# A hybrid decoder layer on one core: another rule for shared SBUF in the kernel's own planner, other planned durations, and three bias buffers in place of two

## The chip, the cores and the metric

The kernel runs on one core of a Trainium2 chip, in one launch. The metric is the device time of that launch in microseconds. The core has five instruction queues that run side by side and meet through semaphores: TensorE (PE; matmuls, with its weight loads shown as PEld), VectorE (DVE), ScalarE (ACT), GpSimd (POOL) and SyncE (SP, which here only issues DMAs). Each queue runs its instructions in the order in which the program issues them, so an instruction that waits holds up all that stand behind it on its engine.

## The reference

One layer on a sequence of 512 tokens with 1024 channels, in fp32. One input projection feeds two attention mixers; their outputs are gated, projected, merged and projected again:

```
h = rms_norm(x, norm_w);  proj = h @ w_in
q_a, k_a, v_a, z_a, q_b, kc, vc, ksl, vsl, kwn, vwn, gate_b, z_b, gate_m = split(proj)
o_a = moba_mixer(norm(q_a), norm(k_a), v_a, bias_a)              # 8 heads of 64
k_cmp = norm(compress(kc)); v_cmp = compress(vc)                 # 31 windows of 32 tokens, gelu MLP
o_b = nsa_mixer(norm(q_b), k_cmp, v_cmp, norm(ksl), vsl, norm(kwn), vwn, gate_b, bias_b)  # 8 heads, 2 groups
y_a = o_a * silu(z_a); y_b = o_b * silu(z_b); g_m = sigmoid(gate_m)
merged = g_m[:1024] * (y_a @ w_branch_a) + g_m[1024:] * (y_b @ w_branch_b)
out = x + merged @ w_out
```

At 512 tokens the block selections of both mixers take in every past block, so the first mixer is causal attention with a relative-position bias, and the second is the gated sum of three attentions with the same queries: over the 31 compressed windows, over the selected keys and over the window keys. The last two share the bias of their head.

## The kernel before

All products are made in fp32r with split operands: an operand is a rounded part (`wh`, `hh`, `ks`, `ph`: "hi") and the remainder (`wl`, `hl`, `kx`, `pl`: "lo"), and a product is three matmuls (hi hi, lo hi, hi lo; `mm3`, L382 to L396) or two. So every weight tile of 128x512 that SP loads (`wr`) costs a cast on ACT or POOL (L359, L363) and a subtraction on DVE or POOL (L368) before TensorE can use it.

Three streams of matmuls are mixed on TensorE: the projections, gates, branches and the output (`gemms`, L1575), the attention (`attention`, L1296: 24 units, one per head for the first mixer, two per head for the second, its branches `br` 0 and 1), and the compression (`cmp`). A unit makes scores of four row blocks (`qk`, L1011), adds the bias and takes the row maximum on DVE (L1045, output `P` or `p`, from PSUM), exponentiates on ACT (L1058), scales by the reciprocal sum on POOL, or for the first mixer on POOL or ACT (L1066, L1064), transposes on TensorE (L1076), splits the transposed block (`ph` on ACT, L1088, `pl` on DVE, L1090) and multiplies with the values (L1110, into `O`). Each head needs its bias matrix `T`, 128x512, loaded from a table in DRAM by `load_bias` (L807); the pool `T` has two buffers. For an NSA group (four heads) `pre0` (L1196) makes keys, queries and the scores over the compressed windows (`scp`, L1217), and `pre1` the transposes of their weights (`pct`, L1262).

**The planner.** No engine's order is written out by hand. While the program is built, a small model of the chip runs: it keeps a clock `now`, a time `free` at which each engine is next free, and a heap of chains of work. A `Chain` (L172) is a list of operations that follow each other, each with a cost in ns by engine: "A" ACT, "D" DVE, "P" POOL. Small letters mark how an operation uses the SBUF access that DVE and POOL share: "d" is a DVE operation with its inputs in SBUF, "P" a POOL operation that takes part in the same lock, "p" a POOL operation that waits for DVE's lock and takes none. `either(n)` (L160) leaves the choice between "d" and "P". `step` (L215) takes the chain with the earliest time, computes with `ends` (L163) when the operation would end on each engine that may do it, takes the earliest, and issues the instruction on that engine at once. `lock["d"]` and `lock["P"]` hold the end of the last such operation of each side; an operation that finds the other side's lock running is priced to end at that lock's end plus its own length less 55. The streams of matmuls are generators: each yields either a condition (a time, or None while unknown) or the length of what it has issued, and the loop at L1749 takes from those whose condition was met at least a margin ago (`margin`, 600 by default, `CMARGIN` for the compression) the one that has had the least of its share. So durations and locks in the model set the order of instructions on all engines and on SP, where the loads `dma` (L254) are issued in planned order too. Semaphores keep the result right whatever the real durations are.

`room(tag)` (L291) says when a buffer of a pool is free in the model, and `alloc` (L269) takes it; RES (L137) lists these pools with their sizes. The pool `att` (tag `a`) with NATT buffers of 128x512 is not in RES: its buffers are reused in turn. Weight tiles come through `NRAW` = 6 raw buffers.

Of the kernel before, what the change touches and what calls it, by code (L numbers as in the profile page):

```python
# [43 lines left out]
YA = {'g0': (0, 1), 'z1': (2, 3)}  # L44
SEQ = ("z0","g0","z1",0,4,"g1",1,5,"g2",2,6,"g3",3,7)
# [6 lines left out]
RAWS = (6, 48)  # L52
# [5 lines left out]
CMARGIN = 2500  # L58
PCT = 2500
# [48 lines left out]
def hybrid_kernel(ctx: ExitStack, tc: tile.TileContext, x, x0, xT, wtok, wchan, wz, wgate, gains, w1,  # L108
# [14 lines left out]
    def nm(s):  # L123
# [14 lines left out]
           "ph": (sp, 3), "P": (sp, 2), "p0": (sp, 2), "T": (sp, 2), "pf": (sp, 2)}  # L138
# [33 lines left out]
    class Chain:  # L172
# [42 lines left out]
        def step(c):  # L215
# [10 lines left out]
            if cost is None:  # L226
                fn()
            else:
                if now[0] > 30e3:
                    cost = {k: n * SLOW[k.upper()] for k, n in cost.items()}  # L230
                end, k = min((ends(k, c.t, n), k) for k, n in cost.items())
                wait = free[k.upper()] - 40 - c.t
                if wait > 0 and c.slack > 0:
                    c.slack -= wait
                    c.t += wait
                    c.push()
                    return
                if k in lock:
                    lock[k] = end
                free[k.upper()] = end  # L240
                c.t = end + OUT[k.upper()] + LAT
                fn(ENG[k])
# [73 lines left out]

    def later(f, d):
        def g():
            t = f()
            return None if t is None else t + d  # L320
        return g
# [252 lines left out]
    def sum_weights():  # L574
# [3 lines left out]
        def both(t, i, k, j, lead):  # L578
# [3 lines left out]
            Chain(t + lead).do({"p": 900}, lambda e: e.dma_start(out=o, in_=y, accum_op=ALU.add, max_dma_last_dim=2048))  # L582
# [236 lines left out]
    def compress_w(kv):  # L819
# [3 lines left out]
        def emit(ps):  # L823
# [10 lines left out]
            for i8 in range(2):  # L834
                XW = att("XW", F32).rearrange("p (i g c) -> p i g c", g=2, c=C32)
                ch.do({"p": 140}, lambda e, XW=XW: e.memset(XW[:, :, :, 31:32], 0.0))
                for g in range(2):
                    ch.do(either(248), lambda e, XW=XW, g=g, i8=i8: e.tensor_tensor(
                        XW[:, :, g, 0:31], b["X"][:, g, :].rearrange("p (c i) -> p i c", i=8)[:, :, i8:i8 + 31],
                        pos[:, kv, 8 * i8:8 * i8 + 8].unsqueeze(2).to_broadcast([P, 8, 31]), op=ALU.add),  # L840
                        (lambda: b["X"]) if i8 and g else None)
# [114 lines left out]
    def q_pair(box, name, col):  # L956
# [5 lines left out]
        for r, z in enumerate(qs):  # L962
            c.do({"A": 478}, lambda e, r=r, z=z: e.copy(z[0:64, :], pt[64 * r:64 * r + 64, :]))
        for r, z in enumerate(qs):
            c.do({"D": 602}, lambda e, r=r, z=z: e.tensor_sub(z[64:128, :], pt[64 * r:64 * r + 64, :], z[0:64, :].bitcast(F32)),
# [3 lines left out]
    def k_pair(boxes, name, col, firsts=None):  # L969
# [6 lines left out]
        for r, (ks, kx) in enumerate(kk):  # L976
            for i in range(2):
                c.do({"A": 478}, lambda e, r=r, z=ks[64 * i:64 * i + 64, :]: e.copy(z, pt[64 * r:64 * r + 64, :]))
        for r, (ks, kx) in enumerate(kk):
            c.do({"D": 602}, lambda e, r=r, ks=ks, kx=kx: e.tensor_sub(  # L980
                kx[0:64, :], pt[64 * r:64 * r + 64, :], ks[0:64, :].bitcast(F32)), pt if r else None)
        for r, (ks, kx) in enumerate(kk):
            c.do({"A": ca(512)}, lambda e, kx=kx: e.copy(kx[64:128, :], kx[0:64, :].bitcast(F32)))
# [9 lines left out]
    class Unit:  # L993
# [44 lines left out]
        def bias(u, c, b, sps, frees, T, last=False):  # L1038
# [10 lines left out]
            c.do({"D": cd(L)}, f, frees, "p0" if own else None)  # L1049
# [4 lines left out]
        def soft(u, c, b):  # L1054
# [12 lines left out]
            p = {"P": 315 + 0.834 * L}  # L1067
# [56 lines left out]
    def o_out(O, m, h):  # L1124
# [11 lines left out]
        ch.do({"A": 478}, f, None, "gmt")  # L1136
# [4 lines left out]
        ch.do({"D": 602}, f, lambda: z["t"])  # L1141
# [44 lines left out]
    def nsa_units(g):  # L1186
# [3 lines left out]
        def bias_now():  # L1190
            if ("T", 0) not in box:
                t = room("T")()
                if t is not None and t <= now[0]:
                    box["T", 0] = load_bias(8 + 4 * g)

        def pre0():  # L1196
            yield toks_of("kb")
            bias_now()
# [7 lines left out]
            bias_now()  # L1206
            yield need("cmpk")
            bias_now()
            sc = att("sc", F32).rearrange("p (i b c) -> p i b c", i=4, b=NT)
            for i in range(4):  # L1210
                q, qc = box["q"][i]
                yield qc.ready
                bias_now()
# [36 lines left out]
            if ("T", 0) not in box:  # L1250
                yield room("T")
                bias_now()

        def pre1():
            yield toks_of("vb")
            yield need("cmpv")
            yield later(box["pcc"].ready, PCT)
# [317 lines left out]
    def gemms():  # L1575
# [26 lines left out]
        pools = [alloc("T", "m", dt=F32R) for _ in range(2)] + [alloc("ph", "m", dt=F32R) for _ in range(3)]  # L1602
# [238 lines left out]
```

## Time and profile before

| | us |
|---|---|
| median of 3 runs | 452.92 (452.29 to 455.07) |
| the profiled execution, its own time | 452.21 |
| its span, first to last instruction | 450.1 |
| granted TensorE clock in it | 1.00 in every slice |
| HBM traffic | 282 GB/s over the span |
| bias loads `T` | 16, each 256 KB |

In the quoted rows a time without a unit is in microseconds. A row of the timeline has start, length, engine, line, operation, output<-inputs, size and count; brackets at its end show for how long its engine had been idle just before, and what ended that. A row of the costliest groups has the count, then busy time and the mean ns of one, then idle time before them and its releasers. A row of one line's instructions has minimum, median and maximum ns of one, then the first and last start. The letter q behind an engine means its queue, where DMAs are issued.

### The profile page before, as it was taken

To read this page: it belongs to the slowest core of one execution; us is meant where nothing else is said; L and a number is where in the kernel's file an instruction comes from. 1 tells how busy PE (TensorE), PEld (TensorE's weight loads), DVE (VectorE), ACT (ScalarE), POOL (GpSimd) and SP (SyncE) were. 2 spreads that over 40 slices of the span, in tenths; PEclk is the share of its full clock that TensorE was granted. 3 is DMA by queue.
4 is the path that set the end of the run, shared out by engine and by line. 5 is a ranking of instruction groups with operands and counts; after the bars stand their busy time and mean duration, and the time that the engine had idled before them with its cause. 6 is when DMAs were issued, how large, how long until landed. Compare 5 with 4: busy or idle time off the path is not lost.

```text
span 450.1 us, 8540 instructions
## 1 busy us (share of the span) xinstructions
PE 442.9 (98%) x2779; PEld 394.5 (88%) x2779; DVE 386.8 (86%) x949; ACT 302.4 (67%) x712; POOL 189.9 (42%) x226
## 2 busy tenths in 40 slices
PE   8999999999999999999899999999999999999996
PEld 7888888899888998889799999989899998998885
DVE  5999899889996789897899999889887699999873
ACT  6775778879998896657686856667664455555450
POOL 1254337747763454335565463647731051211000
PEclk9999999999999999999999999999999999999999
DMA  7886646878876869859967867958769979799862
GB/s 257 284 279 212 217 150 201 212 218 227 237 211 162 223 161 299 281 142 283 248 160 197 231 167 194 238 132 210 176 169 255 264 204 269 216 247 291 302 208 93
DMA packets 54220, 98.20 MB, mean 218 GB/s; under 512 B 5216, under 2 KB 8160, under 8 KB 54176
## 3 DMA queue, kind: packets, MB, share of 16 engines
q1 hardware_dynamic: 38944, 68.30, 47.0%
q0 software_dynamic: 7616, 14.68, 20.2%
q10 hardware_dynamic: 7616, 14.68, 9.8%
q8 instruction: 22, 0.36, 0.3%
q14 instruction: 22, 0.18, 0.1%
HBM read 90.69 MB, written 36.31 MB: 282 GB/s over the span
## 4 chain that ended last, share of the span: by engine, by line
PE 78%; DVE 11%; ACT 4%; issue 3%; DMA 3%; POOL 0%; SPq 0%; ACTq 0%; DVEq 0%
PE pgw L393 16%; PE pgt L393 14%; PE po L393 8%; PE pbr L393 8%; PE pgc L393 6%; PE O L1110 6%; PE pgf L675 5%; PE pt L1076 5%; DVE wl L368 3%; PE sps L1024 3%; PE sps L1025 2%; DMA wr<-in_wgate 2%; DVE P L1045 1%; DVE pl L1090 1%; ACT P L1058 1%
## 5 line engine op out<-in xcount | busy, mean ns | idle before, releaser
L368 DVE TENSOR_TENSOR wl<-wr,wh 128x512 fp32r<-128x512 f32 (+1 forms) x158 | 110.3, 713 | 4.1 <-ACT wh L359 2.9
L359 ACT CAST wh<-wr 128x512 fp32r<-128x512 f32 (+1 forms) x121 | 72.2, 611 | 15.9 <-DMA wr<-wsum 6.5
L1066 POOL TENSOR_SCALAR P<-P,sst,gate 128x512 f32<-128x512 f32 (+3 forms) x56 | 44.6, 799 | 57.8 <-DVE sst L1060 45.5
L363 POOL TENSOR_SCALAR wh<-wr 128x512 fp32r<-128x512 f32 (+1 forms) x48 | 38.2, 801 | 67.2 <-DMA wr<-wsum 20.0
L1058 ACT ACTIVATE P<-P,sst 128x512 f32<-128x512 f32 (+3 forms) x88 | 51.0, 580 | 11.6 <-DVE sst L1045 9.7
L393 PE MATMUL pgt<-wh,hh 128*128 128x512 f32 (+2 forms) x160 | 56.5, 353 | 0.4 <-DVE X L832 0.4
L393 PE MATMUL pgt<-wl,hh 128*128 128x512 f32 (+2 forms) x160 | 55.8, 349 | 0.0
L393 PE MATMUL pgt<-wh,hl 128*128 128x512 f32 (+2 forms) x160 | 55.7, 348 | 0.0
L1045 DVE CUSTOM_DVE_ANT_0 P<-sps,T 128x512 f32<-128x512 f32 (+3 forms) x88 | 43.9, 500 | 10.5 <-PE sps L1025 7.7
L393 PE MATMUL pgw<-th,wh 128*128 128x256 f32 x240 | 48.8, 282 | 0.1
L393 PE MATMUL pgw<-hh,wh 128*128 128x256 f32 x160 | 45.7, 285 | 0.2 <-ACT c L1472 0.2
L1088 ACT CAST ph<-pt 128x512 fp32r<-128x512 f32 (+2 forms) x72 | 33.6, 475 | 17.8 <-PE pt L1076 17.0
L393 PE MATMUL pgw<-hh,wl 128*128 128x256 f32 x160 | 44.4, 278 | 0.0
L393 PE MATMUL pgw<-hl,wh 128*128 128x256 f32 x160 | 44.4, 278 | 0.0
L1076 PE MATMUL pt<-cst,P 128*128 128x128 f32 x232 | 40.9, 273 | 0.5 <-POOL P L1066 0.5
L1090 DVE TENSOR_TENSOR pl<-pt,ph 128x512 fp32r<-128x512 f32 (+2 forms) x72 | 38.8, 548 | 2.3 <-ACT ph L1088 2.1
L393 PEld LDWEIGHTS pgw<-th,wh 128*128 128x128 f32 x240 | 39.1, 188 | 1.2 <-DVE gm L1531 0.5
L434 POOL TENSOR_TENSOR nr<-nss,mhalf 128x8 f32<-128x8 f32 (+1 forms) x16 | 28.7, 1792 | 25.1 <-DVE nss L433 19.5
L1076 PEld LDWEIGHTS pt<-cst,P 128*128 128x128 f32 x232 | 28.9, 140 | 5.5 <-POOL P L1066 0.9
L393 PEld LDWEIGHTS pgt<-wh,hh 128*128 128x128 f32 x160 | 30.1, 188 | 4.0 <-PE hps L862 0.5
L393 PEld LDWEIGHTS pgt<-wl,hh 128*128 128x128 f32 x160 | 30.1, 188 | 3.9
L393 PE MATMUL pgw<-th,wl 128*128 128x256 f32 x120 | 33.2, 277 | 0.0
(269 smaller groups left out, 1275.6 us busy)
## 6 DMA issues: line engine op xcount, KB each, us to landing
wr<-wsum SPq DMA_DIRECT2D x56, 256.0 KB, 4.9
wr<-in_wtok SPq DMA_DIRECT2D x36, 256.0 KB, 5.1
wsum<-in_wgate ACTq DMA_DIRECT2D x16, 512.0 KB, 4.8
wsum<-wsum POOLq DMA_DIRECT2D x14, 512.0 KB, 8.0
wr<-in_wgate SPq DMA_DIRECT2D x24, 256.0 KB, 4.7
xsum<-th SPq DMA_DIRECT2D x16, 256.0 KB, 2.4
T<-rtab SPq DMA_DIRECT2D x16, 256.0 KB, 4.7
wr<-in_w SPq DMA_DIRECT2D x16, 256.0 KB, 4.1
```

Source lines behind the costliest of these rows:

```text
L359: e.copy(hi, raw)
L363: e.tensor_scalar(hi, raw, 1.0, 1.0, op0=ALU.mult, op1=ALU.mult)
L368: c.do({"D": cd(n)} if lead else either(n), lambda e, hi=hi, lo=lo, raw=raw: e.tensor_sub(lo, raw, hi.bitcast(F32))).mark((w, 1, i))
L393: nc.tensor.matmul(dst, sts[i][a], mvs[i][b], start=(start and i == a == b == 0), stop=(stop and i == n - 1 and b == 1), skip_group_check= ...
L434: c.do({"p": 430 + POWC * w}, lambda e: e.tensor_tensor(v(dst), v(ss), mhalf[:parts, :w], op=ALU.pow))
L1045: e.tensor_tensor_reduce(u.block(b), sps[:, :L], T[:, S - L:], scale=-1.0, scalar=3e38, op0=ALU.add, op1=ALU.min, accum_out=st[:, 0, b:b + 1])
L1058: c.do({"A": 279 + 0.834 * L}, lambda e: e.activation(pv(), pv(), AF.Exp, bias=st[:, 0, b:b + 1], scale=-1.0, accum_out=st[:, 1, b:b + 1]))
L1066: e.tensor_scalar(pv(), pv(), st[:, 2, b:b + 1], g, op0=ALU.mult, op1=ALU.mult)
L1076: nc.tensor.transpose(pt[:, (b - kb) * P:(b - kb + 1) * P], u.p0 if u.p0 is not None and b == 0 else u.pb[:, POFF[b] + kb * P:POFF[b] + (k ...
L1088: e.copy(z["w"][0], pt[:, :w])
L1090: ch.do({"D": cd(w)}, lambda e: e.tensor_sub(z["w"][1], pt[:, :w], z["w"][0].bitcast(F32)), pt)
L1110: nc.tensor.matmul(O[0][:, S - n:], v.bitcast(F32) if kb == 3 else v, w, start=(u.first and kb == 0 and i == 0), stop=(u.last and kb == 3 ...
```

## The change

A planned operation that takes part in the lock and finds the other side holding it, while its own side's last such operation ended more than 30 ns before, is not issued: its chain goes back into the heap at the time at which the other side's lock ends, and engine and time are worked out anew then. Further operations of the other side may be planned in between and carry the lock on.

A number of planned durations get other values: two forms of split and copy between halves of the partitions, the addition `XW`, the POOL scaling, the bias operation. The accumulating DMAs that POOL issues get the kind "P" in place of "p", and 680 in place of 900 ns. CMARGIN goes from 2500 to 1000, and the extra delay of 2500 ahead of the transposes in `pre1` goes with its helper.

The pool `T` gets three buffers, `att` 47 in place of 48; the last stage uses the three `T` buffers as spare tiles in place of two. In `pre0` the bias of the group's first head is no longer loaded at the first of five places where a buffer is free, but once, at the end.

```
@@
-RAWS = (6, 48)
+RAWS = (6, 47)
...
-CMARGIN = 2500
-PCT = 2500
+CMARGIN = 1000
...
-           "ph": (sp, 3), "P": (sp, 2), "p0": (sp, 2), "T": (sp, 2), "pf": (sp, 2)}
+           "ph": (sp, 3), "P": (sp, 2), "p0": (sp, 2), "T": (sp, 3), "pf": (sp, 2)}
@@ step
                     c.t += wait
                     c.push()
                     return
+                o = "d" if k == "P" else "P"
+                st = max(c.t, free[k.upper()])
+                if k in lock and lock[o] > st + 1 and lock[k] < st - 30 :
+                    c.t = lock[o]
+                    c.push()
+                    return
                 if k in lock:
                     lock[k] = end
@@
-    def later(f, d):
...
@@ sum_weights
-            Chain(t + lead).do({"p": 900}, lambda e: e.dma_start(out=o, in_=y, accum_op=ALU.add, max_dma_last_dim=2048))
+            Chain(t + lead).do({"P": 680}, lambda e: e.dma_start(out=o, in_=y, accum_op=ALU.add, max_dma_last_dim=2048))
@@ compress_w
-                    ch.do(either(248), lambda e, XW=XW, g=g, i8=i8: e.tensor_tensor(
+                    ch.do({"d": 536, "P": cg(248)}, lambda e, XW=XW, g=g, i8=i8: e.tensor_tensor(
@@ q_pair
-            c.do({"A": 478}, lambda e, r=r, z=z: e.copy(z[0:64, :], pt[64 * r:64 * r + 64, :]))
+            c.do({"A": 590 if r else 482}, lambda e, r=r, z=z: e.copy(z[0:64, :], pt[64 * r:64 * r + 64, :]))
...
-            c.do({"D": 602}, lambda e, r=r, z=z: e.tensor_sub(z[64:128, :], pt[64 * r:64 * r + 64, :], z[0:64, :].bitcast(F32)),
+            c.do({"D": 715}, lambda e, r=r, z=z: e.tensor_sub(z[64:128, :], pt[64 * r:64 * r + 64, :], z[0:64, :].bitcast(F32)),
@@ k_pair
-                c.do({"A": 478}, lambda e, r=r, z=ks[64 * i:64 * i + 64, :]: e.copy(z, pt[64 * r:64 * r + 64, :]))
+                c.do({"A": 482 if i == r else 592}, lambda e, r=r, z=ks[64 * i:64 * i + 64, :]: e.copy(z, pt[64 * r:64 * r + 64, :]))
...
-            c.do({"D": 602}, lambda e, r=r, ks=ks, kx=kx: e.tensor_sub(
+            c.do({"D": 715 if r else 602}, lambda e, r=r, ks=ks, kx=kx: e.tensor_sub(
...
-            c.do({"A": ca(512)}, lambda e, kx=kx: e.copy(kx[64:128, :], kx[0:64, :].bitcast(F32)))
+            c.do({"A": 110 + ca(512)}, lambda e, kx=kx: e.copy(kx[64:128, :], kx[0:64, :].bitcast(F32)))
@@ Unit.bias, Unit.soft
-            c.do({"D": cd(L)}, f, frees, "p0" if own else None)
+            c.do({"D": cd(L) + 10}, f, frees, "p0" if own else None)
...
-            p = {"P": 315 + 0.834 * L}
+            p = {"P": 270 + 0.79 * L}
@@ o_out
-        ch.do({"A": 478}, f, None, "gmt")
+        ch.do({"A": 590}, f, None, "gmt")
...
-        ch.do({"D": 602}, f, lambda: z["t"])
+        ch.do({"D": 711 if row else 602}, f, lambda: z["t"])
@@ nsa_units
-        def bias_now():
-            if ("T", 0) not in box:
-                t = room("T")()
-                if t is not None and t <= now[0]:
-                    box["T", 0] = load_bias(8 + 4 * g)
...
-            bias_now()
...
-            if ("T", 0) not in box:
-                yield room("T")
-                bias_now()
+            yield room("T")
+            box["T", 0] = load_bias(8 + 4 * g)
...
-            yield later(box["pcc"].ready, PCT)
+            yield box["pcc"].ready
@@ gemms
-        pools = [alloc("T", "m", dt=F32R) for _ in range(2)] + [alloc("ph", "m", dt=F32R) for _ in range(3)]
+        pools = [alloc("T", "m", dt=F32R) for _ in range(3)] + [alloc("ph", "m", dt=F32R) for _ in range(3)]
```

More of the change, by code (lines that the diff above doesn't have):

```diff
@@ L43 @@
 YB = {"g3": (0, 1), 6: (2, 3)}
-YA = {'g0': (0, 1), 'z1': (2, 3)}
-SEQ = ("z0","g0","z1",0,4,"g1",1,5,"g2",2,6,"g3",3,7)
+YA = {"g0": (0, 1), "z1": (2, 3)}
+SEQ = ("z0", "g0", "z1", 0, 4, "g1", 1, 5, "g2", 2, 6, "g3", 3, 7)
 ASUM = 62e3
@@ L314, in all_of @@
         return f
-    def later(f, d):
[L318 to L321, printed above, removed]
     W1_ = [None]
@@ L1205, in pre0 @@
                 yield from q_pair(box["q"], "qb", 256 * g + P * i)
-            bias_now()
             yield need("cmpk")
-            bias_now()
             sc = att("sc", F32).rearrange("p (i b c) -> p i b c", i=4, b=NT)
@@ L1212, in pre0 @@
                 yield qc.ready
-                bias_now()
                 yield room("s")
@@ L1249, in pre0 @@
             box["pcc"] = cc
-            if ("T", 0) not in box:
-                yield room("T")
-                bias_now()
+            yield room("T")
+            box["T", 0] = load_bias(8 + 4 * g)
         def pre1():
```

## The prediction

> **What bounds the kernel now.** I read the page's shares first, then the chain that ended last, then the busy time by stage.
>
> ```profile
> PE 442.9 (98%) x2779; PEld 394.5 (88%) x2779; DVE 386.8 (86%) x949; ACT 302.4 (67%) x712; POOL 189.9 (42%) x226
> PE 78%; DVE 11%; ACT 4%; issue 3%; DMA 3%; POOL 0%; SPq 0%; ACTq 0%; DVEq 0%
> 0.00:4.72 4.72, 3.49 (x31) 3.25 (x32) 0.80 (x3) 2.29 (x4) 0.55 (x8) 1.00 0.59 148
> 4.72:60.00 55.28, 55.28 (x246) 45.54 (x247) 49.13 (x98) 37.93 (x76) 19.33 (x21) 1.00 0.76 255
> 60.00:200.00 140.00, 139.53 (x853) 122.38 (x853) 124.46 (x336) 114.39 (x277) 76.78 (x84) 1.00 0.78 213
> 200.00:240.00 40.00, 38.24 (x271) 34.86 (x270) 34.79 (x98) 29.23 (x80) 23.83 (x31) 1.00 0.77 204
> 240.00:400.00 160.00, 159.76 (x1156) 149.11 (x1155) 141.48 (x354) 98.81 (x244) 66.50 (x80) 1.00 0.81 213
> 36.04 0.39 PE L393 MATMUL pgt<-wl,hh 128*128 128x512 f32 x1
> 36.27 0.39 PE L393 MATMUL pgt<-wh,hh 128*128 128x512 f32 x1
> ```
>
> The second line is the share of each engine in the chain, the next five are stages (length, then busy PE, PEld, DVE, ACT, POOL, the granted clock, the DMA share and GB/s). TensorE is the bound, at the full granted clock. Its idle time between the first weights and the last stage is 140.00-139.53 = 0.47, 40.00-38.24 = 1.76 and 160.00-159.76 = 0.24: 2.47 us. The last two rows say that this is too little: neighbouring matmuls start 0.23 us apart while each is shown 0.39 long, so every wait is 0.16 longer than its idle row, and waits under 0.16 don't show. With some fifteen waits (an estimate) the whole is about 2.5 + 15 x 0.16 = 5 us. That is all a better order of instructions can win: the change leaves the matmuls, the head and the last products alone. What it can lose has no such limit. The profiled execution took 452.21 us: 450.1 of span and 2.1 around it. The median of the three runs, 452.92, is 0.7 above it.
>
> **The change, part 1: who holds SBUF.** Nothing is added to the program; the planner orders it differently. A planned operation of kind "d" or "P" that finds the other engine holding SBUF, and whose own engine has not just used it, is now put off to the end of that hold and chosen anew; before, it was issued at once and priced as starting 55 ns before that end. Is the hold real?
>
> ```profile
> 366.80 3.24 POOL L363 TENSOR_SCALAR wh<-wr 128x512 fp32r<-128x512 f32 x1 [4.43 <-DVE ma L1368]
> 366.66 0.69 DVE L368 TENSOR_TENSOR wl<-wr,wh 128x512 fp32r<-128x512 f32 x1
> 368.87 0.69 DVE L368 TENSOR_TENSOR wl<-wr,wh 128x512 fp32r<-128x512 f32 x1
> 370.74 1.84 POOL L363 TENSOR_SCALAR wh<-wr 128x512 fp32r<-128x512 f32 x2
> 370.83 1.27 DVE L1524 TENSOR_TENSOR gm<-gm,R 128x512 f32<-128x512 f32 x1
> 372.03 1.09 DVE L368 TENSOR_TENSOR wl<-wr,wh 128x512 fp32r<-128x512 f32 x1
> L363 POOL TENSOR_SCALAR wh<-wr x48: 592/622/3241, 7.7 to 400.8; 128x512 fp32r<-128x512 f32 x45, 128x280 fp32r<-128x280 f32 x3
> ```
>
> The same POOL operation has a median of 622 ns and once took 3.24 us: while six DVE operations with both inputs in SBUF (the first and the last are shown) followed each other without a gap, it did not get in once. Where POOL itself came straight from another operation (370.74, two in 1.84), the engines took turns: DVE's 1.27 and 1.09 are a 0.69 operation and a wait for POOL. The new test, with its exception for an engine that has just held SBUF, says both. [...]
>
> What the better price is worth is seen where TensorE waits.
>
> ```profile
> 216.49 1.30 POOL L368 TENSOR_TENSOR wl<-wr,wh 128x512 fp32r<-128x512 f32 x1
> 216.87 1.47 DVE L368 TENSOR_TENSOR wl<-wr,wh 128x512 fp32r<-128x512 f32 x1
> 218.26 0.41 DVE L1045 CUSTOM_DVE_ANT_0 P<-sps,T 128x256 f32<-128x256 f32 x1
> 218.60 0.88 DVE L1090 TENSOR_TENSOR pl<-pt,ph 128x384 fp32r<-128x384 f32 x2
> 219.20 0.44 PE L1110 MATMUL O<-pl,vb 128*128 128x384 f32 x1 [0.84 <-DVE pl L1090]
> 219.65 1.55 POOL L1066 TENSOR_SCALAR P<-P,sst,gate 128x384 f32<-128x384 f32 x2 [1.87 <-DVE sst L1060]
> 221.26 0.55 PE L1076 MATMUL pt<-cst,P 128*128 128x128 f32 x3 [0.54 <-POOL P L1066]
> ```
>
> POOL held SBUF from 216.49 to 217.8; DVE's split at 216.87 was queued behind it and blocked, and with it the bias and `pl` behind it on DVE, which read PSUM and needed no part of the hold. TensorE then waited 0.84 for `pl`. With the new test that split is put off to 217.8 and the two go first, 1.4 us earlier: the 0.84 goes. The other 0.92 of the 1.76 is of mixed cause (0.54 is a POOL scaling), and I take half: -0.84-0.46 = -1.30. Of the 0.47+0.24 elsewhere I take half, -0.35, and 3 waits x 0.16 hidden, -0.48. What is late next is DVE: 34.79 of 40 us busy there, so a plan that orders it otherwise cannot empty it. Bounds of this part: -5 (all waits) to 0, or above: it can also push POOL's work to DVE and ACT. If all twelve splits that POOL now makes (the row below) went to DVE at 0.69 each, that is 8.3 us, against 400-350.7 = 49 us of DVE idle time before 400 (0.80+49.13+124.46+34.79+141.48 = 350.7): covered, except at 200-240, where each would cost up to its 0.69.
>
> ```profile
> L368 POOL TENSOR_TENSOR wl<-wr,wh x12: 783/1300/2396, 66.5 to 271.3; 128x512 fp32r<-128x512 f32 x9, 128x280 fp32r<-128x280 f32 x3
> ```
>
> **Part 2: measured durations.** They change no instruction, only the plan's clock.
>
> ```profile
> L965 DVE TENSOR_TENSOR qs<-pq,qs 64x512 fp32r<-64x512 f32 x16 | 11.0, 690 | 1.6 <-ACT qs L963 1.2
> L963 ACT CAST qs<-pq 64x512 fp32r<-64x512 f32 x16 | 9.3, 582 | 2.7 <-PE pq L947 2.5
> L1066 POOL TENSOR_SCALAR P<-P,sst,gate 128x512 f32<-128x512 f32 x16 | 14.5, 903 | 38.9 <-DVE sst L1060 26.7 <-PE sps L1025 8.3 <-PE pt L1076 3.6
> L582 POOL DMA_DIRECT2D wsum<-wsum x14 | 12.9, 921 | 5.3 <-DMA wsum<-wsum 5.3
> ```
>
> 602 becomes 715 (row: 690), 478 becomes 482 or 590 (582): nearer. The scaling goes from 742 to 674 at 512 columns, further from 903; POOL's DMA issue from 900 to 680 (row: 921), and it now takes part in the hold. I set this part to 0: right in two, wrong in two. At most each of the 28 issues (the loops of `sum_weights`) plans POOL 0.2 early, 5.6 us in all, on an engine that is 42% busy; the lower end is the same with the sign turned.
>
> **Part 3: three bias buffers, loads later.** The early load in `pre0` (`bias_now`, five places) goes; the bias of each NSA group is now asked for behind all scores, and a third buffer takes the place of one of 48 in the pool `att`.
>
> ```profile
> T<-rtab SPq DMA_DIRECT2D x16, 256.0 KB, 4.7
> DMA to landing us min/median/max: 3.7/4.7/7.5
> 196.38 5.03 SPq L256 DMA_DIRECT2D T<-rtab  x2
> 169.03 0.53 SPq L256 DMA_DIRECT2D T<-rtab  x1
> 178.17 1.13 PE L1217 MATMUL scp<-kcs,qs 128*128 128x64 f32 x8
> 181.76 0.69 DVE L1045 CUSTOM_DVE_ANT_0 P<-sps,T 128x512 f32<-128x512 f32 x1
> 240.80 0.53 SPq L256 DMA_DIRECT2D T<-rtab  x1
> 259.76 0.53 PE L1217 MATMUL scp<-kcs,qs 128*128 128x64 f32 x4
> 262.93 0.69 DVE L1045 CUSTOM_DVE_ANT_0 P<-sps,T 128x512 f32<-128x512 f32 x1
> 250.00:275.00 25.00, 24.96 (x180) 23.24 (x179) 24.03 (x70) 19.09 (x51) 14.29 (x16) 1.00 0.71 178
> ```
>
> Gain: with two buffers a bias load stood at the head of SP's queue from 196.4 to 200.9 until DVE released a buffer, and the weight loads behind it stood too. TensorE did not wait for a weight there, so I count 0. Loss: the groups' first biases were loaded at 169.03 and 240.80, 12.7 and 22.1 us ahead of use at 181.76 and 262.93. Behind the last scores (end about 179.1 and 260.1) plus 4.7 they land at 183.8 and 264.8: 2.0 and 1.9 late if the rest stays where it is. DVE's bias waits, and behind it on DVE the weight splits that TensorE needs some tiles later. After 250 DVE has 25.00-24.03 = 0.97 idle in 25 us, so 0.9 of the second can come through; I take +0.5. Bounds: 0 (the plan has other work first) to what the longest landing gives, 179.1+7.5-181.8 = 4.8 and 260.1+7.5-262.9 = 4.7. The one `att` buffer less I set to 0: the last stage gets it back as a third spare tile; the bound is one reload held back, 4.7 by the nearest load row.
>
> **Part 4: two margins.** The compression matmuls may now start 1.0 instead of 2.5 us after the plan thinks their input is ready, and the extra 2.5 ahead of the transposes `pct` goes, so an error of the plan reaches TensorE sooner.
>
> ```profile
>   DVE vl L368: 0.2, 1
>   ACT ch L954: 4.9, 2
> ```
>
> These are the compression's only wait for DVE, 0.2 us once, and the followers of `pct` (ACT, 4.9 in two waits, nobody's bound). Sixteen weight tiles at up to 0.2 are 3.2 us; I take +0.3, and 0 as the lower end.
>
> **Sum**, against 452.21: -1.30-0.35-0.48+0.5+0.3 = -1.33, so 450.9. From the median of 452.92 the same step gives 451.6. I forecast between them: 451.2 us.
>
> **Rivals.** (a) All waits go: 452.2-5 = 447.2. For it: the largest waits lie in one stage with a cause that the new test names. Against: DVE is 87% busy there and causes most of them. (b) The change does not do what it says: the holds over several operations hit nothing on the path (at 366.80, where POOL lost 2.6 us, stage 240-400 has 0.24 of TensorE idle in all), and the new order wins and loses alike: 452.5. [...] (c) Slower: the late bias at the start of the NSA groups takes the place of the waits removed. At the longest landing the two are 4.8 and 4.7 late. DVE can make up 0.97 of the second, and of the first 2.8 (its idle share in 60-200 is 15.5 of 140, over 25 us): 2.0+3.7 = 5.7, with nothing won, 457.9. It decides once the plan puts the first NSA bias less than a landing behind the last score; for it speaks that DVE runs in order and nothing but that bias guards its place, against it that the plan itself adds about 2.7 us for this load, so only the rest is a surprise.
>
> **How the numbers follow.** Forecast (half the waits go, 449.5 to 452.2) 0.46; (a) 0.08; (b) 0.24; (c) 0.22, half of it near its full price. The range reaches to (a) and to (c): 447.6 to 456.8 leaves 2 in 10 out; the likeliest case alone has 449.5 to 452.2. About 1%, 4.5 us, is what can be told from no change here. Faster by over that (below 448.4): (a) and a little of the forecast, 0.12. Slower (over 457.4): 0.15, from (c) and from orders that I don't see. Within: 0.73.
>
> **What would show it.** Right: in the stage around 200-240 TensorE's idle time falls from 1.76 to below 1; no POOL operation of 0.6 takes over 2 us; DVE has fewer splits of over 1 us; the last two bias loads of a group stand no longer at SP's head. Wrong: idle time of DVE ahead of the bias line L1045 just behind the scores, ended by a DMA of `T`; new TensorE waits on `vl` or `pcs`; a TensorE idle sum above 2.5 us outside the head and the last stage.

## The result and the profile after

The changed kernel takes 457.92 us (median of four, 457.38 to 460.36), the kernel before 452.87 beside it: a ratio of 1.0112, with a 95% interval of 1.0084 to 1.014. It is 5.05 us slower, where 451.2 was forecast. The profiled execution took 458.30, with a span of 456.4 against 450.1. In the code after the change lines up to about L1190 stand one lower than before, later ones twelve lower.

The busy time by engine, from the page of the profile:

```profile
PE 442.2 (97%) x2779; PEld 394.1 (86%) x2779; DVE 387.0 (85%) x950; ACT 302.7 (66%) x709; POOL 187.8 (41%) x228
```

Every engine is busy for as long as before, within 2.1 us. What grew is TensorE's idle time, from 7.2 us (450.1-442.9) to 14.2 (456.4-442.2); that covers the 6.3 us of span. By stage (start:end, length, then busy time of PE, PEld, DVE, ACT, POOL, clock, DMA share, GB/s):

```profile
4.72:60.00 55.28, 54.63 (x247) 44.88 (x247) 48.17 (x100) 38.28 (x77) 17.90 (x19) 1.00 0.77 258
60.00:200.00 140.00, 134.81 (x821) 118.02 (x820) 121.88 (x323) 107.82 (x261) 76.05 (x88) 1.00 0.77 210
200.00:240.00 40.00, 38.38 (x270) 35.35 (x269) 33.80 (x102) 30.24 (x84) 25.50 (x31) 1.00 0.75 198
240.00:400.00 160.00, 158.52 (x1142) 147.54 (x1141) 139.56 (x350) 100.67 (x245) 64.35 (x79) 1.00 0.80 208
```

Idle time is length less busy time: 0.65, 5.19, 1.62 and 1.48, where it was 0, 0.47, 1.76 and 0.24. The sum, outside the head and the last stage, is 8.94, where it was 2.47. The stage on which the forecast rested, 200 to 240, gained 0.14; the one that had nothing left to win, 60 to 200, lost 4.72. What TensorE waited for, before (engine, tile, line, releaser: us in all, times, longest):

```profile
PE O L1110 <- DVE pl L1090: 1.2, 2, 0.8
PE pw L456 <- POOL ones L407: 0.9, 1, 0.9
PE pt L1076 <- POOL P L1066: 0.5, 1, 0.5
PE pgt L393 <- DVE X L832: 0.4, 1, 0.4
PE pgf L675 <- DVE wh L361: 0.4, 1, 0.4
PE pgw L393 <- ACT c L1472: 0.2, 1, 0.2
```

The same view after the change:

```profile
PE pt L1075 <- POOL P L1065: 2.3, 2, 1.6
PE pt L1075 <- DVE sst L1059: 1.9, 2, 1.6
PE sps L1023 <- DVE sst L1044: 1.7, 1, 1.7
PE pt L1075 <- DVE qs L964: 1.0, 2, 0.7
PE pw L455 <- POOL ones L406: 0.9, 1, 0.9
PE hps L862 <- DVE vl L367: 0.7, 1, 0.7
PE pgf L674 <- POOL wh L362: 0.6, 1, 0.6
PE pgw L392 <- ACT c L1460: 0.6, 1, 0.6
PE pgf L674 <- DVE wh L360: 0.2, 1, 0.2
PE pt L1075 <- DVE kx L979: 0.2, 1, 0.2
```

The sums are 3.6 and 10.1, so 6.5 more, about the 6.3 of the span. The two waits for `pl` (1.2), the ones the change was to remove, are gone. In their place stand waits of the transposes `pt` for POOL's scaling or for an operation of DVE (`sst`, `qs`), of the scores `sps` for DVE, and of `hps` for a weight split. The waits that DVE ends went from 2.0 to 5.7. The timeline shows how the three longest come about:

```profile
90.92 0.95 POOL L581 DMA_DIRECT2D wsum<-in_wz  x1
91.62 1.58 POOL L367 TENSOR_TENSOR vl<-wr,vh 128x512 fp32r<-128x512 f32 x1
91.43 2.07 DVE L367 TENSOR_TENSOR wl<-wr,wh 128x280 fp32r<-128x280 f32 x1
94.51 0.38 PE L1023 MATMUL sps<-ks,qs 128*128 128x256 f32 x1 [1.75 <-DVE sst L1044]
163.65 1.60 POOL L367 TENSOR_TENSOR wl<-wr,wh 128x512 fp32r<-128x512 f32 x1
164.02 1.77 DVE L367 TENSOR_TENSOR vl<-wr,vh 128x512 fp32r<-128x512 f32 x1
168.45 0.52 PE L1075 MATMUL pt<-cst,P 128*128 128x128 f32 x3 [1.62 <-DVE sst L1059]
221.06 5.67 POOL L1065 TENSOR_SCALAR P<-P,sst,gate 128x384 f32<-128x384 f32 x3 [1.19 <-DVE sst L1059]
223.67 1.88 DVE L367 TENSOR_TENSOR wl<-wr,wh 128x512 fp32r<-128x512 f32 x3
226.04 0.55 PE L1075 MATMUL pt<-cst,P 128*128 128x128 f32 x3 [1.62 <-POOL P L1065]
```

In the first two a DVE split ends just behind the POOL split beside it, at 93.50 us (POOL at 93.20) and at 165.79 (POOL at 165.25): 2.07 us for an operation whose shortest row on this line is 0.42, 1.77 for one with a median of 0.68. The next DVE operations start at 93.43 and 165.83 us, so the bias operation (93.77) and the sums (168.22) come late, and TensorE stands. In the third it is the other way round: three POOL scalings take 5.67 where the mean of their line is 862 ns, and three splits follow each other on DVE meanwhile. So the contention that the new test was to plan around stands behind the three longest waits of the new order, 5.0 of the 10.1; whether they would go without it is asked further down, with the order held fixed. The experiments ask whether the test, another part, or the redrawing of the order itself brought it.

### The profile page after: what moved, and what is told of

Same layout as the page of the kernel before. It is cut to its first block, busy times and chain, and to the rows that moved or that the text cites. A ratio compares the mean times of both kernels' runs of the same rounds, so it can differ in the third digit from the quotient of the medians.

```text
span 456.4 us, 8530 instructions
## 1 busy us (share of the span) xinstructions
PE 442.2 (97%) x2779; PEld 394.1 (86%) x2779; DVE 387.0 (85%) x950; ACT 302.7 (66%) x709; POOL 187.8 (41%) x228
## 4 chain that ended last, share of the span: by engine, by line
PE 81%; DVE 9%; DMA 5%; POOL 2%; issue 2%; ACT 1%; SPq 0%; ACTq 0%; DVEq 0%
PE pgt L392 18%; PE pgw L392 17%; PE pbr L392 9%; PE po L392 8%; PE pgc L392 6%; PE O L1109 5%; PE pt L1075 4%; PE pgf L674 4%; PE sps L1023 3%; PE sps L1024 2%; POOL P L1065 2%; DMA wr<-in_wgate 2%; DVE P L1044 1%; DMA xsum<-th 1%; DVE vl L367 1%
## 5 line engine op out<-in xcount | busy, mean ns | idle before, releaser
L367 DVE TENSOR_TENSOR wl<-wr,wh 128x512 fp32r<-128x512 f32 (+1 forms) x158 | 107.5, 698 | 2.0 <-ACT wh L358 1.1
L358 ACT CAST wh<-wr 128x512 fp32r<-128x512 f32 (+1 forms) x125 | 74.2, 610 | 16.5 <-DMA wr<-in_wtok 4.4
L1065 POOL TENSOR_SCALAR P<-P,sst,gate 128x512 f32<-128x512 f32 (+3 forms) x56 | 47.8, 862 | 57.0 <-DVE sst L1059 42.0
L362 POOL TENSOR_SCALAR wh<-wr 128x512 fp32r<-128x512 f32 (+1 forms) x44 | 35.0, 802 | 68.2 <-PE pgw L392 27.6
L433 POOL TENSOR_TENSOR nr<-nss,mhalf 128x8 f32<-128x8 f32 (+1 forms) x16 | 26.9, 1682 | 23.8 <-DVE nss L432 18.1
L392 PEld LDWEIGHTS pgt<-wh,hl 128*128 128x128 f32 x160 | 30.1, 188 | 3.3
```

The source lines that it names most:

```text
L358: e.copy(hi, raw)
L362: e.tensor_scalar(hi, raw, 1.0, 1.0, op0=ALU.mult, op1=ALU.mult)
L367: c.do({"D": cd(n)} if lead else either(n), lambda e, hi=hi, lo=lo, raw=raw: e.tensor_sub(lo, raw, hi.bitcast(F32))).mark((w, 1, i))
L392: nc.tensor.matmul(dst, sts[i][a], mvs[i][b], start=(start and i == a == b == 0), stop=(stop and i == n - 1 and b == 1), skip_group_check= ...
L433: c.do({"p": 430 + POWC * w}, lambda e: e.tensor_tensor(v(dst), v(ss), mhalf[:parts, :w], op=ALU.pow))
L1065: e.tensor_scalar(pv(), pv(), st[:, 2, b:b + 1], g, op0=ALU.mult, op1=ALU.mult)
```

## The experiments

The change has four parts: **M**, both margins (`CMARGIN` and the delay ahead of `pct`); **H**, the test who holds SBUF; **T**, three bias buffers with the late load; **D**, the durations. Without M none of the other three was tried on the kernel before. Each time is a median beside runs of the kernel before on the same chip (452.6 to 453.7), with the ratio to it and its interval.

### The parts

Before with M, alone and with one part beside it. The first edit:

```
-CMARGIN = 2500
+CMARGIN = 1000
...
-            yield later(box["pcc"].ready, PCT)
+            yield box["pcc"].ready
```

> Before with the two margins alone (compression 1000 in place of 2500, no extra 2500 ahead of the transposes pct). Theory 'hold' (the loss of 5.05 us comes from the new rule for SBUF, which puts POOL and DVE against each other at the wrong places): no change, 452 to 454 us. Theory 'any new order' (the order of before was a lucky one, and whatever makes the planner order anew loses some us): slower, 455 to 459. Theory 'margin' (matmuls issued before their input is there): slower by most of the 5, 456 to 458, with TensorE waiting on vl in the compression.

Measured: 462.23, ratio 1.02 [1.0162, 1.0238].

With H besides:

```
+                o = "d" if k == "P" else "P"
+                st = max(c.t, free[k.upper()])
+                if k in lock and lock[o] > st + 1 and lock[k] < st - 30 :
+                    c.t = lock[o]
+                    c.push()
+                    return
```

> Before with the margins and the new rule for SBUF. Theory 'hold': close to the changed kernel, 456 to 460 us, with DVE operations of over 1.7 us behind POOL and POOL scalings of over 2.2 us. Theory 'any new order': slower than before, 454 to 460, without relation to the first. Theory 'late bias': as the margins alone, 452 to 454.

Measured: 457.85, ratio 1.0109 [1.0073, 1.0146].

M with T (the pools, and `bias_now` gone; some of its lines):

```
-RAWS = (6, 48)
+RAWS = (6, 47)
...
-            if ("T", 0) not in box:
-                yield room("T")
-                bias_now()
+            yield room("T")
+            box["T", 0] = load_bias(8 + 4 * g)
...
```

> Before with the margins and the three bias buffers with their late load. Theory 'late bias': 456 to 458 us, with DVE idle ahead of the bias line at the start of the two NSA groups, ended by a DMA. Theory 'hold': as the margins alone, 452 to 454. Theory 'any new order': 454 to 460.

Measured: 465.77, ratio 1.0293 [1.0228, 1.0358].

M with D (all the durations; one for the rest):

```
-            p = {"P": 315 + 0.834 * L}
+            p = {"P": 270 + 0.79 * L}
```

> Before with the margins and the new durations (with the lock for POOL's DMA issues). Theory 'hold': as the margins alone, 452 to 454 us. Theory 'any new order': 454 to 460. A theory 'too cheap scaling' (POOL's scaling planned 0.07 us shorter, so the transposes are issued too soon): slower by 2 to 4, with TensorE waiting on POOL's scaling.

Measured: 457.83, ratio 1.0105 [1.0074, 1.0137].

From the other end, the changed kernel without T, and then without D (one line for the rest in each):

```
-           "ph": (sp, 3), "P": (sp, 2), "p0": (sp, 2), "T": (sp, 3), "pf": (sp, 2)}
+           "ph": (sp, 3), "P": (sp, 2), "p0": (sp, 2), "T": (sp, 2), "pf": (sp, 2)}
```

> The change without its third part: two bias buffers, 48 buffers in att, the early bias load. Theory 'late bias' (that part costs, as from 462.2 to 465.8 between the kernels with the margins alone and with the margins and the biases): 453 to 456 us. Theory 'any new order' (each order is a draw, about 452 to 466, and only a part's mean over several orders means something): 453 to 463, on either side of the changed kernel's 457.9.

Measured: 461.63, ratio 1.0192 [1.0152, 1.0232].

```
-            p = {"P": 270 + 0.79 * L}
+            p = {"P": 315 + 0.834 * L}
```

> The change without the new durations (and with the old lock for POOL's DMA issues). Set against the kernel with margins and biases (465.8) it shows the rule for SBUF once more: theory 'the rule helps' (with the margins alone it brought 462.2 to 457.9): 459 to 463 us, with less blocked time of DVE and POOL than there. Theory 'hold' (the rule is the loss): 466 or more. Theory 'any new order': 453 to 466.

Measured: 462.98, ratio 1.0219 [1.0176, 1.0263].

What follows: beside M, none of the other parts has a price of its own, or even a sign. H takes 4.4 from M alone (462.23 to 457.85) and 2.8 from M with T (465.77 to 462.98), but adds 3.8 to M with D (457.83 to 461.63). D takes 4.4 from M and 5.1 from M with H and T (462.98 to 457.92), but adds 3.8 to M with H. T adds 3.5 to M and takes 3.7 from M with H and D. By the intervals such a difference is known to some 2 to 4 us, so the 2.8 could be nothing, and T's 3.5 only just is not; the changes of sign of H and of D are clear. The differences do not add up.

### The margins

They are the two values that every run so far shares. One at a time on the kernel before: `CMARGIN` alone, then the delay alone.

```
-CMARGIN = 2500
+CMARGIN = 1000
```

> Before with the compression's margin alone, 1000 in place of 2500. Theory 'compression margin' (the 8.5 us that both margins cost come from compression matmuls that are issued too early): 459 to 463 us. Theory 'transposes' (they come from the extra delay of 2500 that is gone): 452 to 454. Theory 'any new order': 455 to 460, like any other edit.

Measured: 460.88, ratio 1.0179 [1.0135, 1.0222].

```
-            yield later(box["pcc"].ready, PCT)
+            yield box["pcc"].ready
```

> Before without the extra 2500 ahead of the transposes pct, the compression's margin kept. TensorE's order is the same up to some 190 us. Theory 'compression margin': 452 to 454 us. Theory 'transposes': 459 to 463, with TensorE waiting at the first pct. Theory 'any new order': 454 to 460.

Measured: 450.12, ratio 0.9951 [0.9932, 0.9971]: faster than both kernels. Up to about 200 us its TensorE order is that of before. In its profile two of the waits between 200 and 240 us are gone (TensorE is idle there for 0.80 instead of 1.76), but three new ones stand behind 360, so where its 2.5 us come from stays open.

So the margin of the compression seemed to be the loss. If it is, a value between must lie between, and the changed kernel with nearly the old margin must be near the time before:

```
-CMARGIN = 1000
+CMARGIN = 2300
```

> The changed kernel with the compression's margin at 2300 in place of 1000. Theory 'compression margin': TensorE's waits at 80 to 175 us fall to the 3 us of the kernel before, and the time to 452 to 455 us. Theory 'any new order': 455 to 465, with waits anywhere.

Measured: 460.61, ratio 1.017 [1.0149, 1.0192].

The kernel before, with a margin a fifth smaller:

```
-CMARGIN = 2500
+CMARGIN = 2000
```

> Before with the compression's margin at 2000 in place of 2500. Theory 'compression margin': little of the 8.2 us that 1000 costs, so 453 to 456 us, with the extra waits at 100 to 150. Theory 'any new order': 455 to 462, with waits anywhere.

Measured: 463.54, ratio 1.0228 [1.021, 1.0246].

So the price does not follow the size of the margin. Giving back most of it makes the changed kernel 2.7 slower, and on the kernel before a margin of 2.0 us costs more (463.54) than one of 1.0 (460.88). Nor do the compression's own matmuls `hps` stand among TensorE's waits in the run with `CMARGIN` alone; the largest there are waits of `pt`, 1.8 for POOL's scaling and 1.7 for `qs`. One thing is not excluded: that any shorter margin costs some us on the average, by way of the order. All twelve redrawn orders here that have one, at 1.0, 2.0 or 2.3 us, take 457.83 or more, and no run has H, T and D with the old margin.

### Edits that mean nothing

If any redrawing costs, an edit with no physical content must cost as well. Four of them: the planned start of the weight sums 0.1 us later, on both kernels; the planned length of the small power operation on POOL longer by 5 ns per column (it has 4 or 8 columns); a latency constant of the plan 2 ns longer.

```
-ASUM = 62e3
+ASUM = 62.1e3
```

> Before with the weight sums planned 0.1 us later (62.1 in place of 62): an edit that means nothing, and orders TensorE's instructions anew from the first quarter on. Theory 'any new order': 455 to 460 us. All other theories: 452 to 454.

Measured, on the kernel before: 454.95, ratio 1.0053 [1.0033, 1.0072].

```
-POWC = 180
+POWC = 185
```

> Before with POOL's power planned 5 ns longer per column: again an edit that means nothing, and a new order from the first tenth on. Theory 'any new order': 455 to 460 us, and not the same as the other nudge. All other theories: 452 to 454.

Measured, on the kernel before: 458.76, ratio 1.0112 [1.0067, 1.0157].

```
-ASUM = 62e3
+ASUM = 62.1e3
```

> The changed kernel with the weight sums planned 0.1 us later, an edit that means nothing. Theory 'any new order': other than 457.9 by 1 to 5 us, on either side. Theory 'the parts set the time': 457 to 459.

Measured, on the changed kernel: 462.36, ratio to the kernel before 1.0188 [1.0146, 1.0231].

```
-LAT = 60
+LAT = 62
```

> The changed kernel with each planned hand-over between engines 2 ns longer, an edit that means next to nothing and orders nearly everything anew. Theory 'any new order': other than 457.9 by 1 to 5 us, on either side. Theory 'the parts set the time': 457 to 459.

Measured, on the changed kernel: 464.37, ratio 1.0249 [1.0191, 1.0306].

These nudges cost 2.3 and 6.1 us on the kernel before (from 452.63) and 4.4 and 6.5 on the changed one. The change's own 5.05 is of that size, and 20 to 40 ns in one planned duration give the same ratio, 1.0112; that the two ratios agree to the last digit is chance. All the redrawn orders together, the changed kernel among them, are fifteen: from 450.12 to 465.77, with a median of 460.88. One is faster than before. The changed kernel is fifth of the fifteen; the order before is simply better than nearly all that its planner draws when something is moved. The fifteen are not independent draws, as twelve of them share a shorter margin; of the three that keep the old one, one is faster (450.12) and two are slower (454.95, 458.76), and only the last of these is redrawn early. In five of these runs (e1, e3, e5, e12, e18) the time lies above the range that the theory 'any new order' gave, in two (e6, and e7 by 0.05) below it.

Does the new rule make orders better on the average? Seven runs have it (e2, e9 to e12, e17 and the change): mean 461.1. Of those without it, six are redrawn early (e1, e3, e4, e5, e8, e18): mean 461.5. Left out are the two whose TensorE order stays with the old one for long, e6 to about 200 us and e7 to about 155. The difference of 0.4 is nothing against a spread of 6 to 8 us on either side.

### The order held fixed

What does the new order lose physically? Here the order is frozen, so that only the hardware's part changes (TensorE's matmuls follow each other in the same order, tile by tile, as in the kernel that each run starts from). In the first of these POOL's splits and products with two inputs read one input, in the same places; in the second POOL's scaling of the attention weights is left out; the third does both, and the fourth does both to the kernel before.

```
-                c.do({"D": cd(n)} if lead else either(n), lambda e, hi=hi, lo=lo, raw=raw: e.tensor_sub(lo, raw, hi.bitcast(F32))).mark((w, 1, i))
+                c.do({"D": cd(n)} if lead else either(n), lambda e, hi=hi, lo=lo, raw=raw: one_in(e, lambda e: e.tensor_sub(lo, raw, hi.bitcast(F32)), lo, hi.bitcast(F32))).mark((w, 1, i))
...
+    def one_in(e, two, dst, src):
+        if e is nc.gpsimd:
+            e.tensor_scalar(dst, src, 1.0, 1.0, op0=ALU.mult, op1=ALU.mult)
+        else:
+            two(e)
...
```

> The changed kernel in its own order on all engines; POOL's two-input operations on weights and gated outputs read one input only (it leaves out their subtraction or product), so they are about half as long and DVE waits less behind them. Theory 'contention by POOL's long operations' (the waits at 94.5, 168.4, 169.4 and 243.5 us, 4.9 us in all, come from DVE held up by a POOL operation of 1.3 to 1.6): 453 to 455 us. Theory 'something else': 457 to 458.

Measured: 455.75, ratio 1.007 [1.0048, 1.0093].

```
-                    e.tensor_scalar(pv(), pv(), st[:, 2, b:b + 1], g, op0=ALU.mult, op1=ALU.mult)
+                    pass
```

> The changed kernel in its own order; the scaling of the attention weights on POOL is left out (ACT's share of it stays). Theory 'starved scalings' (the waits at 226.0 and 286.9 us, 2.6 us, come from POOL kept out by a run of DVE splits): 454.5 to 456 us. Theory 'something else': 457 to 458.

Measured: 456.89, ratio 1.0093 [1.006, 1.0126].

Both edits, on the changed kernel:

> The changed kernel in its own order with both left out, POOL's two-input forms and its scalings. Theory 'contention' in full: 449 to 452 us, so within 2 of the kernel before treated the same way. Theory 'something else': over 455, and about 5 above the kernel before treated the same way.

Measured: 452.24, ratio 0.9998 [0.9971, 1.0024].

Both edits, on the kernel before:

> The kernel before in its own order with both left out. Its waits at 219.2 and 221.3 us (1.7) go: 449.5 to 451.5 us by theory 'contention', since its order has little of it on the path; 452 to 453 by 'something else'.

Measured: 449.09, ratio 0.993 [0.9902, 0.9958].

All four times miss the ranges of the theories that blame POOL, by 0.2 to 0.9 us: the first three are slower than foreseen, the last is faster. With both left out, the two kernels still are 3.15 apart, where 2 at most was foreseen. Alone the two edits give 2.2 and 1.0 us, together 5.7. That is 2.5 more than their sum, about as much as the intervals of the four times leave open; the traces show how it can come about, as a wait that goes lets another grow or stay. In the first, the wait at 94.5 falls from 1.75 to 1.11, but the one at 168.4 stays, at 1.51 for 1.62: its split takes 1.09 in place of 1.77 and starts after 0.51 of waiting for a cast on POOL. In the second, the `pt` wait at 243.5, 0.66 in the changed kernel, has become 1.78, with the same releaser, DVE's `qs` (timeline of that kernel):

```profile
243.70 0.55 PE L1075 MATMUL pt<-cst,P 128*128 128x128 f32 x3 [1.78 <-DVE qs L964]
```

POOL's share in what the new order loses, its contention with DVE and the length of its scaling, is therefore 5.7 us; in the old order it is 3.8 (452.89 to 449.09). Of the 5.05 between the kernels it explains 5.7-3.8 = 1.9, a difference that the intervals (some 1.2 us to either side of each time) do not set clear of nothing. The other 3.15 stay, clear of noise, and most of them lie where the loss lay. The changed order without POOL's share, as a row of the stages (TensorE alone):

```profile
60.00:200.00 140.00, 136.31 (x832) 1.00 0.78 211
```

Its three largest waits at `pt`, `sps` and `hps`:

```profile
PE pt L1081 <- DVE sst L1065: 1.1, 2, 0.8
PE sps L1029 <- DVE sst L1050: 0.8, 1, 0.8
PE hps L868 <- DVE vl L373: 0.7, 1, 0.7
```

And its timeline behind the third:

```profile
106.44 0.91 POOL L587 DMA_DIRECT2D wsum<-wsum  x1
107.08 1.09 POOL L843 TENSOR_TENSOR XW<-X,cst 128x248 f32<-128x248 f32 x1
107.24 2.06 DVE L373 TENSOR_TENSOR vl<-wr,vh 128x512 fp32r<-128x512 f32 x1
```

The order before, with the same left out:

```profile
60.00:200.00 140.00, 139.21 (x855) 1.00 0.77 212
```

Between 60 and 200 us TensorE is idle for 3.69 in the one and 0.79 in the other, 2.9 more, the largest difference of any stage. (These two profiled executions are 5.55 apart, 453.61 and 448.06, so the 2.9 is not a share of the 3.15 between the medians.) The same three waits are still the largest there, halved or whole: 0.76, 0.84 and 0.72, where they were 1.75, 1.62 and 0.69. Part of what is left is contention too, of a kind that these edits do not touch: the split at 107.24 takes 2.06 behind POOL's DMA issue, its `XW` and the cast that follows at 107.80. How much of the 3.15 is that, and how much plain lateness of DVE in this order, stays open.

## Why the prediction was wrong

The forecast has the wrong sign, and 457.92 lies above the range's upper end of 456.8.

**The step that failed** is the basis of the sum: "against 452.21: -1.30-0.35-0.48+0.5+0.3". It takes the order before as given and subtracts the waits that the new test removes from it. But no edit tried on this planner left the rest of the order alone: those without meaning moved the time by 2.3 to 6.5 us. The prediction knew that what a better order can win is bounded (5 us) and that what it can lose "has no such limit"; yet the losses in its sum, +0.5 and +0.3, and the one of (c) are priced in the old order, waits of a new order stand in the sum at nothing, and all of slower than 457.4, "orders that I don't see" included, got 0.15. With fourteen of fifteen redrawn orders slower, that term was the likeliest case and the largest of all. In the changed kernel it is the 4.72 us by which TensorE's idle time between 60 and 200 grew, where the forecast had a gain. Open is how much of it any shorter margin would cost, and why exactly DVE is late there.

**Part 1, the hold.** The mechanism is there. The named wait of 0.84 for `pl` is gone, and the hold over several operations recurs in the new order (5.67 us for three scalings, the timeline above). The size failed: -1.30 was expected at 200 to 240, and -0.14 came, as the wait of 1.62 at 226.04 took the place of the two for `pl`. The -0.35-0.48 elsewhere came as a gain nowhere: idle time outside 200 to 240 rose. "What is late next is DVE" was right: DVE ends most of the new waits. Its sign "DVE has fewer splits of over 1 us" came, six where there were at least eight, and yet says little, as three of the six take 1.77 to 2.07, longer than any before. The lines of DVE's splits, the kernel before:

```profile
L368 DVE TENSOR_TENSOR wl<-wr,wh x158: 436/685/1465, 5.4 to 441.0; 128x512 fp32r<-128x512 f32 x153, 128x280 fp32r<-128x280 f32 x5
L368 DVE TENSOR_TENSOR vl<-wr,vh x16: 666/682/1044, 82.8 to 172.9; 128x512 fp32r<-128x512 f32 x16
```

The changed kernel:

```profile
L367 DVE TENSOR_TENSOR wl<-wr,wh x158: 420/684/2074, 5.3 to 447.3; 128x512 fp32r<-128x512 f32 x152, 128x280 fp32r<-128x280 f32 x6
L367 DVE TENSOR_TENSOR vl<-wr,vh x14: 675/683/2032, 83.2 to 164.0; 128x512 fp32r<-128x512 f32 x14
L362 POOL TENSOR_SCALAR wh<-wr x44: 422/624/2125, 6.9 to 408.2; 128x512 fp32r<-128x512 f32 x42, 128x280 fp32r<-128x280 f32 x2
```

Minimum, median and maximum in ns: DVE's longest split went from 1465 to 2074, that of `vl` from 1044 to 2032, while the medians stayed. POOL's longest cast fell from 3241 to 2125, and still is over 2 us. A plan that knows of the hold did not keep clear of it. One reason may be that the test looks only at a hold that is already planned when an operation is drawn, and the operations that lengthen it can be drawn later; that was not tried by itself.

A single split of DVE overlaps more than one POOL instruction in the runs: that of 2.07 us (91.43) a DMA issue and a split (90.92 and 91.62), the one of 2.06 with POOL's share left out (107.24) `XW` and a cast (107.08 and 107.80). The bias operation, which reads PSUM, keeps its length beside POOL, as the prediction had it: in the kernel before one of 384 columns takes 0.55 us in the median of the six rows that lie wholly inside a power, a scaling or a split of POOL, and 0.56 in that of the nine that overlap nothing of POOL.

**Part 2, the durations, 0.** No sign of its own, as expected; but beside M it moves the time by -4.4, -5.1 or +3.8 by redrawing. That the bound of 5.6 us, worked out from POOL's DMA issues, is of this size is chance. The scaling's 903 ns, against which the planned 674 was judged further off, is a mean with waits in it: of the seventeen rows of one scaling of 512 columns in the kernel before, eleven took 0.69 to 0.78 us.

**Part 3, the biases, +0.5.** Here the expected loss did not come. In the view of the tile `T` the changed kernel has these causes of DVE's idle time ahead of the bias operation (us, times), and this time from a load's issue to its landing:

```profile
  PE sps L1024: 11.6, 18
  POOL P L1065: 1.1, 1
DMA to landing us min/median/max: 3.7/5.8/11.1
```

No DMA is among them, though loads took longer than before (a median of 5.8 against 4.7). The second group's first bias shows why:

```profile
261.98 1.06 PE L1206 MATMUL scp<-kcs,qs 128*128 128x64 f32 x8
262.42 0.66 SPq L261 DMA_DIRECT2D T<-rtab  x1
268.74 0.69 DVE L1044 CUSTOM_DVE_ANT_0 P<-sps,T 128x512 f32<-128x512 f32 x1
```

The load is issued beside the last scores, and the first use stands 5.7 us behind the end of those scores (261.98+1.06 to 268.74), where the old order had 2.6 (259.76+0.53 to 262.93): the use moved with the load. Rival (c) had the right side and nearly the right time, 457.9, but its mechanism was not seen; the agreement of the number is chance. It, too, priced one wait in a fixed order.

**Part 4, the margins, +0.3.** "An error of the plan reaches TensorE sooner" was priced by the waits that were already there. By themselves the two values gave +8.2 (460.88 against 452.63) and -2.5. This is the term most wrong in size. It does not come from the wait that the prediction priced, TensorE's for `vl`: with `CMARGIN` alone none stands in the list of TensorE's waits, and in the changed kernel there is one of 0.69 (a sign of being wrong that did come). And a margin of 2.0 us costs more than one of 1.0.

**Rivals (a) and (b).** The bound of 5 us for a gain is not contradicted: the best order seen wins 2.5. (b) had the right thought, "the new order wins and loses alike", and the wrong centre: an order that is better than most loses, on the average, when it is drawn again.

## What to carry to other kernels

Where one planner writes the whole order, an edit of its model is a new draw of everything behind it; before crediting or blaming the edit, time a few nudges without meaning, and compare it with their spread (here +2.3 to +6.5 us of 453), not with the one order that happens to be in use. Idle rows bound what such an edit can win; what it can lose is bounded by nothing in the profile of the old order, and if that order is already nearly free of waits, a loss is the likelier outcome. A contention that costs little in one order (here 3.8 us) need not cost the same in another (5.7, though the intervals leave the difference open): freeze the order to price it, and do not expect the prices of two cures to add up.

## What the runs showed of the hardware

**TensorE's clock fell to half in stretches of 3.41 us, and before most of these TensorE had been idle for about half of the 3.41 us or more.** In the kernel before the granted clock was 1.00 in every slice. In ten of the fifteen redrawn orders the profile has stretches at 0.50, and a mean clock of 0.987 to 0.996. In the run with the longer power operation one follows a single long wait (a row of the timeline):

```profile
298.15 0.39 PE L1024 MATMUL sps<-ks,qs 128*128 128x256 f32 x1 [2.07 <-DVE sst L1045]
```

The 3.41 us before the stretch, and the stretch (TensorE's busy time alone, then clock, DMA share, GB/s):

```profile
296.15:299.56 3.41, 1.41 (x8) 1.00 0.14 46
299.56:302.97 3.41, 3.41 (x13) 0.50 0.49 154
```

In the run with `CMARGIN` alone two shorter waits, of 1.23 and 0.53, stand before one:

```profile
108.73 0.33 PE L1076 MATMUL pt<-cst,P 128*128 128x128 f32 x1 [1.23 <-DVE qs L965]
109.94 0.63 PE L947 MATMUL pq<-cst,qk 128*128 128x128 f32 x4 [0.53 <-DVE pl L1090]
107.05:110.46 3.41, 1.65 (x12) 1.00 0.97 153
110.46:113.87 3.41, 3.41 (x17) 0.50 0.56 176
```

The run with the longer latency constant has a wait of 1.94 (ended at 269.32) with a stretch of 3.41 us, and a longer one with a stretch of twice that:

```profile
130.40 0.58 PE L1023 MATMUL sps<-ks,qs 128*128 128x256 f32 x1 [3.06 <-DVE sst L1044]
129.36:136.19 6.83, 5.79 (x19) 0.50 0.71 215
```

A stretch costs half of itself, 1.7 us for 3.41, on top of the waits. This is an estimate, for matmuls that follow each other without a gap, from the clock of 0.50 and from rows of 128x256: they start 0.21 and 0.22 us apart inside a stretch (250.97, 251.18 and 251.40 in the change without its third part) and 0.11 and 0.13 apart at 1.00 (266.19, 266.30 and 266.43 in the run with the longer latency). In the profiles there are thirteen (one of them in the first run with the order held fixed). In the 3.41 us before twelve of them TensorE is idle for 1.7 to 3.0 us (2.00 with the longer power operation, 1.76 with `CMARGIN` alone, 2.02 and 1.93 with the longer latency, 2.97 in the change without its third part); before the one of the run with both margins the rows show only 0.95, beside narrow products of 64 columns. Single waits of 1.75 (the changed kernel) and 1.78 (above) were not followed by a stretch, nor was one of 1.84 in the run with the longer latency. In the changed kernel TensorE was idle for 1.82 of the 3.41 us up to 169.40 (3.41-1.59), and the clock stayed at 1.00; so no limit comes out of these rows.

The changed kernel shows a mean clock of 0.995 or 0.996 in three of its four executions, which is about one such stretch, and 1.00 in the profiled one. As that one, at 458.30, was no faster, the clock is not where the 5.05 us are.
